# Row tiles in a pool of their own, and other banks and addresses at the start of the down stage

## The chip, the cores and the metric

The kernel runs on one core of one Trainium2 chip. The metric is device time in microseconds (us) for one execution of the whole program; less is better.

## What is computed

Two layers of a decoder trunk on an input x of 1024 rows by 1024 columns, all in float32. Each layer has a mix part (a causal convolution group and a differential attention group side by side, then one projection) and a gated feed-forward part; each adds its normalized result to x:

```python
z = jnp.einsum("bsd,dc->bsc", rms_norm(x, pre_mix_norm[l]), w_in[l])
u, o = conv_group(z), diff_attention_group(z)
m = jnp.einsum("bsc,cd->bsd", jnp.concatenate([u, o], axis=-1), w_out[l])
x = x + rms_norm(m, post_mix_norm[l])
up = jnp.einsum("bsd,df->bsf", rms_norm(x, pre_ffn_norm[l]), w_up[l])
g, val = jnp.split(causal_dwconv(up, ffn_conv_w[l], ffn_conv_b[l]), 2, axis=-1)
f = jnp.einsum("bsf,fd->bsd", jax.nn.gelu(g, approximate=True) * val, w_down[l])
x = x + rms_norm(f, post_ffn_norm[l])
```

The feed-forward width is 2816: w_up has 2 x 2816 columns, w_down 2816 rows.

## The kernel before, in words

Per layer there are three stages on TensorE: **mix**, **up** (w_up with the convolution of width 3 and the gate) and **down** (w_down). A float32 product is made of three float32r products: each operand is split in a high part (a rounded copy by ScalarE, line 1278) and a low part (the operand less the high part, by VectorE or GpSimd, line 1279), and high x high, low x high and high x low are summed in one PSUM bank. Up and down are done by a seven-product scheme (Strassen-like) on halves of the operands, which is why seven pieces f_l_j_k of the gated result are written to DRAM by up (lines 1482, 1484 and 1498, from the tiles gg and fs) and read back by down.

**Mix.** The last thing that it does on each 128-row tile is the post-norm: it fetches the row (xe), adds the normalized projection to it (lines 1165, 1166), stores it (1168), squares it (1171), scales it by the next norm's gain into xn (1178) and transposes it. Row tiles of 1024 columns have the tag e and five slots in the pool mx; the same tag serves the attention's exponentials. bst (statistics) and the query tiles ql1 and ql2 lie in the same pool.

**Up.** It begins with the loads of its convolution weights fw and fb (1269, 1271) and of the first raw weight blocks (1382), which lie where the tiles of the mix stage have been. The parts of a block are the tiles wo (seven slots). The products px, py and pz (line 1582) go to the PSUM pools pO, pS and pmm; VectorE adds them into cg and cv (1450); taps of the convolution are summed in acc (PSUM pools pmm for the gate half, ptr for the value half, 1456 and 1468); line 1478 multiplies acc and vv into gg.

**Down.** `run(j, ps, ...)` (line 1612) does product j of the seven: 11 chunks of 256 KB, each with 12 matmuls (line 1633): four row tiles tt = 0 to 3, each with its own bank ps[tt], by three part products. The operands of a chunk are the parts of a piece of f (fa, loaded by `fetch_f`, line 1550) and of a weight block (wbA, wbB or wb, loaded by `fetch`, line 1545). The parts of the first three chunks' weights are in wo slots, those of all later ones in wp slots (five, pool dn of the down stage). `prepare` (1552) makes the parts three chunks ahead. The banks come from `banks` (1687): product 1 begins in

```python
return ([pmm.tile([P, HB], F32, tag="mm", name="pd") for _ in range(2)]
        + [pS.tile([P, HB], F32, tag="S", name="pd") for _ in range(2)])
```

and four partial sums of 512 columns each, s1, u2 and vv, are kept in SBUF in the pool dn (line 1699), allocated before the wp slots. dn's tiles lie on addresses that tiles of the up stage have had, so the first instruction that writes one waits for the last reader of whatever lay there. The next layer's mix stage lies over dn's tiles in the same way: its first raw blocks (line 454) lie where s1 was; their high parts are whw (458, ScalarE), their low parts wlw (464, GpSimd), and the first products are pg (494).

The order of the instructions on TensorE, VectorE, ScalarE and GpSimd is the order in which the code issues them or, in the mix stage, a planner written out in the kernel. Nearly all DMAs go through one queue, SP, in order: one that waits holds all that stand behind it. A scheduler chooses the place of a DMA in SP's order when the program is built. A row in this text is named by the line numbers of the kernel before.

Of the kernel before, what the change touches and what calls it, by code (L numbers as in the profile page):

```python
# [9 lines left out]
F32 = mybir.dt.float32  # L10
F32R = mybir.dt.float32r
# [6 lines left out]
P = 128  # L18
D = 1024
T = 1024  # L20
DEPTH = 2
HB = 512
# [33 lines left out]
E_BUFS = 5  # L56
# [157 lines left out]
def build(tc, ap, out):  # L214
# [4 lines left out]
    def mv(dst, src):  # L219
        sy.dma_start(f32(dst), f32(src))  # L220

    with ExitStack() as top:
        def pool(st, name, **kw):
            return st.enter_context(tc.tile_pool(name=name, **kw))
# [5 lines left out]
        pmm = pool(top, "pmm", bufs=2, space=PSUM)  # L230
        pS = pool(top, "pS", bufs=3, space=PSUM)
        ptr = pool(top, "ptr", bufs=2, space=PSUM)
        pO = pool(top, "pO", bufs=1, space=PSUM)
# [182 lines left out]
        for l in range(DEPTH):  # L416
            xres = xin if l == 0 else x2[l - 1]
            with ExitStack() as st:
                mx = pool(st, f"mx{l}", bufs=1, reuse_waits="tile")
                mw = pool(st, f"mw{l}", bufs=1, reuse_waits="tile")  # L420
                hh = (hA, hB)
                if l == 0:
                    for t in range(8):
                        late[t] = prenorm(ptr, x0[t] if t < 3 else first_x(t), g_pre, hh[t // 4], t % 4)
                p = params(l)
                wm = ap["wmix"][l]

                bst = mx.tile([P, 8, 4, 6], F32, tag="bst", name="bst")
                qlow = [mx.tile([P, HB], F32R, tag=tag, name=tag) for tag in ("ql1", "ql2")]
                po.memset(f32(qlow[0][64:128]), 0.0)  # L430
                po.memset(f32(qlow[1][0:64]), 0.0)
# [2 lines left out]
                                                     e=E_BUFS, aT=AT_BUFS, osb=1, qs=1, kA=1, kB=1, v0=2, v1=2,  # L434
# [92 lines left out]
                def conv_gate(ct, b, ps, im):  # L527
                    tag = "e" if ct == 0 else "m0"
                    it = yield from R[tag].get()
                    if ct == 0:  # L530
                        tg = mx.tile([P, T], F32, tag="e", name="tg", bufs=E_BUFS)[:, 0:HB]
                    else:
                        tg = xs.tile([P, HB], F32, tag="m0", name="tg", bufs=4)
                    se.activation(tg, ps, AF.Tanh, scale=0.5)
                    t = fl.op("act", ac(HB))
                    R["mm"].free(im, t)
                    tgs[ct, b] = tg, tag, it
                    fl.set("tg", ct, b)
# [256 lines left out]
                def attn(h, b):  # L795

                    n = SEQ.index((h, b))
                    if n > 0:
                        yield ("S", SEQ[n - 1][0], 4 * SEQ[n - 1][1] + 3)
                    if b == 1:  # L800
                        yield ("kA", h)
                    yield ("qk", h, b)
                    q1, q2 = kq[h, b]
                    grp = {}
                    for qb in range(4 * b, 4 * b + 4):
                        nk = (qb + 1) * P
                        qsl = slice(qb % 4 * P, (qb % 4 + 1) * P)
                        both = []
                        for qs, ql, ki in ((q1, qlow[0], 0), (q2, qlow[1], 1)):
                            ie = yield from R["e"].get()  # L810
                            e = mx.tile([P, T], F32, tag="e", name="e", bufs=E_BUFS)
                            pcs = []
                            for c0 in range(0, nk, HB):
                                w = min(HB, nk - c0)
                                iS = yield from R["S"].get()
                                S = pS.tile([P, HB], F32, tag="S", name="S")[:, 0:w]
                                diag = c0 + w == nk
                                kt = kk[h, c0 // HB]
                                pe.matmul(S, qs[:, qsl], kt[ki][:, 0:w], start=True, stop=False)
                                pe.matmul(S, ql[:, qsl], kt[ki][:, 0:w], start=False, stop=not diag)  # L820
                                if diag:
                                    pe.matmul(S[:, w - P:w], identr, nmaskr, start=False, stop=True)  # L822
                                t = fl.op("pe", 2 * max(0.107, w / 2400) + (0.06 if diag else 0))
                                pcs.append((S, c0, w, iS))
                            fl.spawn(soft(h, qb, pcs, e, ie, both, grp), t)
                        if qb % 4 == 3:
                            R["qs"].free(ikq[h, b, "qs"], t)
                            if b == 1:
                                R["kA"].free(ikq[h, 0, "k"], t)
                                R["kB"].free(ikq[h, 1, "k"], t)  # L830
                            elif h in SPILL:
                                R["kA"].free(ikq[h, 0, "k"], t)
                        fl.set("S", h, qb)
# [121 lines left out]
                def norm(h, b, grp):  # L955
                    osb, oss, ep = grp[0]
                    po.tensor_scalar(ep, ep, EPS * P, None, op0=ALU.mult)
                    po.tensor_tensor(ep, ep, oss, op=ALU.add)
                    po.tensor_tensor(ep, ep, negh[:, 0:G], op=ALU.pow)
                    yield fl.op("pool", 1.6)  # L960
                    for qi in range(G):
                        se.activation(osb[:, qi], osb[:, qi], AF.Copy, scale=ep[:, qi:qi + 1])
                        t = fl.op("act", 0.29)
                    yield t
                    io = yield from R["e"].get()
                    onT = mx.tile([P, 2, HB], F32R, tag="e", name="onT", bufs=E_BUFS)
                    ip = yield from R["tr"].get()
                    pt = ptr.tile([P, G, P], F32, tag="tr", name="pto")
                    for qi in range(G):
                        pe.transpose(pt[:, qi], osb[:, qi], ident)  # L970
                    t = fl.op("pe", 0.48)
                    R["osb"].free(grp[1], t)
                    yield t
                    ptf = pt.rearrange("p a b -> p (a b)")
                    se.activation(onT[:, 0], ptf, AF.Copy, scale=p["sg"])
                    t = fl.op("act", ac(HB) + 0.1)
                    yield t
                    ve.scalar_tensor_tensor(onT[:, 1], ptf, p["sg"], f32(onT[:, 0]), op0=ALU.mult, op1=ALU.subtract)
                    t = fl.op("dve", dv(HB), t)
                    R["tr"].free(ip, t)  # L980
                    mv(osp[l][h][b], onT)
                    R["e"].free(io, t + MV_LAT)
                    yield t
                    fl.set("norm", h, b)
# [70 lines left out]
                m0s, xe = {}, {}  # L1055
# [55 lines left out]
                def wout_half(dh, b, tt, ps, tag, im):  # L1111
# [21 lines left out]
                    yield t  # L1133
                    if b == 1:
                        i = yield from R["e"].get()
                        x = mx.tile([P, D], F32, tag="e", name="xe", bufs=E_BUFS)
                        sy.dma_start(x, xres[4 + tt])
                        xe[tt] = x, i, fl.now + MV_LAT
                        fl.set("xe", tt)

                def wout_post(dh, b, tt, ps, tag, im):
# [4 lines left out]
                    if b == 1:  # L1146
                        if ("xe", tt) not in fl.seen:
                            yield ("xe", tt)
                        x, ie, tx = xe[tt]
                        yield from R["xr" if tt < 2 else "y"].get()  # L1150
                        xn = xs.tile([P, D if tt < 2 else YW], F32, tag="xr" if tt < 2 else "y", name="xn", bufs=2)[:, 0:D]
# [56 lines left out]
                        R["y"].free(i, t)  # L1208
                    yield ("hA2",)
                    i = yield from R["e"].get()  # L1210
                    xn = mx.tile([P, D], F32, tag="e", name="xn", bufs=E_BUFS)
                    ss = xs.tile([P, 1], F32, tag="ss", name="ss", bufs=3)
                    se.activation(xn, y, AF.Square, accum_out=ss)
                    t = fl.op("act", ac(D) + 0.1)
# [50 lines left out]
            with ExitStack() as st:  # L1265
# [36 lines left out]
                with ExitStack() as su:  # L1302
# [197 lines left out]
                    for n in range(NFT):  # L1500
                        e, f4 = slot[3, n] + 1, slot[4, n] + 1
# [107 lines left out]
                with ExitStack() as sd:  # L1609
                    dn = pool(sd, f"dn{l}", bufs=1, reuse_waits="tile")  # L1610
# [73 lines left out]
                    def keep(name):  # L1684
                        return [dn.tile([P, HB], F32, tag=name, name=name, bufs=4) for _ in range(4)]

                    def banks(which):
                        if which == 0:
                            return ([pmm.tile([P, HB], F32, tag="mm", name="pd") for _ in range(2)]
                                    + [pS.tile([P, HB], F32, tag="S", name="pd") for _ in range(2)])  # L1690
                        return ([pS.tile([P, HB], F32, tag="S", name="pd"), pO.tile([P, HB], F32, tag="o", name="pd")]
                                + [ptr.tile([P, HB], F32, tag="tr", name="pd") for _ in range(2)])

                    inB = [hpool.tile([P, 8, HB], F32, tag="hB", name="wbB") for _ in range(2)]
# [1 line left out]
                    spB = [t[:, j] for t in inB for j in range(8)]  # L1696
                    B.update({"dn": dn, "12": spB[0:K2], "22": own[1:12], "21": B["A"][K2:16] + spB[K2:16] + own[0:1]})
                    pa = banks(0)
                    s1, u2, vv = keep("s1"), keep("u2"), keep("vv")
                    m0s = {}  # L1700

                    def end1(tt):
# [126 lines left out]
```

## Time and profile before

| | us |
|---|---|
| median of 3 runs | 2388.04 (2386.19 to 2391.40) |
| the profiled execution | 2385.93 |
| its span | 2384.1 |
| TensorE busy | 2214.6 |
| TensorE's mean granted clock | 0.965 of full speed |

A busy line gives the time that an engine worked. A wait is idle time of an engine right before an instruction, with the instruction that ended it. A timeline gives the instructions of an engine in order of time, with consecutive like ones merged. Times in views are us from the start of the span.

### The profile page before, as it was taken

The numbers are of one execution on the slowest core, as the hardware profiler recorded it, in microseconds if no ns is written. First come the engines' busy times: TensorE is split into PE (matmuls) and PEld (weight loads), VectorE is DVE, ScalarE is ACT, GpSimd is POOL, SyncE is SP. The second block draws the span as 40 slices with busy tenths as digits, with TensorE's granted clock in tenths as the row PEclk, the third lists the DMA queues.
The fourth block names the chain that finished last, engine by engine and source line by source line (L and its number), as shares of the span: only waits on it lengthen the run. The fifth ranks groups of instructions, "written<-read, shape, count | busy, mean of one in ns | idle before, by whom it ended". The sixth has DMA issues, their size and how long they took to land. (4 is left out here: it accounts for less than half of the span.)

```text
span 2384.1 us, 31534 instructions
## 1 busy us (share of the span) xinstructions
PE 2214.6 (93%) x10568; PEld 1845.5 (77%) x10568; DVE 1857.6 (78%) x3285; ACT 1132.9 (48%) x2458; POOL 826.0 (35%) x896
## 2 busy tenths in 40 slices
PE   6999998959999999899869999989699999998997
PEld 4998886748877878788658988867588778787886
DVE  6889989537888888677668899885478888886777
ACT  4445556535444444444434455565354544444443
POOL 3223312234544544202432233122354555442024
PEclk9999998979999999999979999989899999999999
DMA  4313323644334334833333123236433334348343
GB/s 144 78 53 89 90 74 114 200 137 143 111 124 132 111 125 152 286 98 102 110 113 80 53 87 93 71 112 202 143 133 124 120 121 135 103 168 273 98 150 106
DMA packets 140129, 295.39 MB, mean 124 GB/s; under 512 B 16832, under 2 KB 33984, under 8 KB 139456
## 3 DMA queue, kind: packets, MB, share of 16 engines
q1 hardware_dynamic: 139968, 293.39, 38.7%
q8 instruction: 83, 1.36, 0.2%
q14 instruction: 78, 0.64, 0.1%
HBM read 198.44 MB, written 78.12 MB: 116 GB/s over the span
## 5 line engine op out<-in xcount | busy, mean ns | idle before, releaser
L1633 PE MATMUL pd<-wp,wo 128*128 128x512 f32 x1776 | 411.3, 393 | 5.5 <-DVE vv L1718 2.9
L1633 PEld LDWEIGHTS pd<-wp,wo 128*128 128x128 f32 x1776 | 336.0, 190 | 77.8 <-issue 3.3
L1582 PE MATMUL py<-t,wo 128*128 128x512 f32 x1584 | 377.5, 391 | 4.5 <-DVE cg L1450 4.5
L1582 PEld LDWEIGHTS py<-t,wo 128*128 128x128 f32 x1584 | 296.6, 188 | 73.4 <-ACT wo L1278 7.7
L1279 POOL TENSOR_TENSOR wo<-ws,wo 128x512 fp32r<-128x512 f32 x176 | 252.2, 1444 | 283.7 <-ACT wo L1278 246.6
L1582 PE MATMUL px<-hA,wo 128*128 128x512 f32 x1056 | 261.6, 400 | 43.4 <-ACT wo L1278 42.3
L1582 PEld LDWEIGHTS px<-hA,wo 128*128 128x128 f32 x1056 | 199.6, 190 | 93.4 <-ACT wo L1278 43.2
L1279 POOL TENSOR_TENSOR wo<-raw,wo 128x512 fp32r<-128x512 f32 x132 | 177.4, 1348 | 145.0 <-ACT wo L1278 142.6
L1279 POOL TENSOR_TENSOR wo<-fa,wo 128x512 fp32r<-128x512 f32 x66 | 101.4, 1552 | 328.2 <-ACT wo L1278 308.6
L1278 ACT ACTIVATE wo<-ws 128x512 fp32r<-128x512 f32 x176 | 108.5, 626 | 135.7 <-PE py L1582 57.4
L1468 DVE SCALAR_TENSOR_TENSOR acc<-cg,fw,acc 128x512 f32<-128x512 f32 x176 | 132.7, 754 | 41.7 <-ACT acc L1456 38.0
L592 DVE SCALAR_TENSOR_TENSOR scr<-u,cw,scr 128x256 f32<-128x256 f32 (+2 forms) x288 | 158.9, 572 | 0.4
L494 PE MATMUL pq<-whq,hA 128*128 128x384 f32 x512 | 138.2, 352 | 5.8 <-ACT whq L458 5.8
L1456 ACT ACTIVATE acc<-cg,fb,fw 128x512 f32<-128x512 f32 x88 | 68.2, 775 | 148.0 <-DVE cg L1450 148.0
L494 PE MATMUL pq<-whq,hB 128*128 128x384 f32 x512 | 135.6, 346 | 0.0
L1582 PE MATMUL pz<-b,wo 128*128 128x512 f32 x528 | 131.1, 397 | 2.0 <-DVE cv L1450 2.0
L1582 PE MATMUL pz<-t,wo 128*128 128x512 f32 x528 | 130.5, 396 | 0.0
L847 ACT ACTIVATE e<-S,mxv 128x512 f32<-128x512 f32 (+2 forms) x192 | 110.0, 581 | 42.9 <-DVE mxv L842 31.7
L838 DVE TENSOR_REDUCE mxv<-S 128x1 f32<-128x512 f32 (+2 forms) x192 | 100.7, 549 | 29.1 <-PE S L822 27.1
L852 POOL TENSOR_TENSOR sm<-sm 128x1 f32<-128x1 f32 x64 | 27.2, 425 | 274.7 <-ACT e L847 274.7
L1582 PEld LDWEIGHTS pz<-b,wo 128*128 128x128 f32 x528 | 98.3, 188 | 28.4 <-issue 5.4
L1582 PEld LDWEIGHTS pz<-t,wo 128*128 128x128 f32 x528 | 99.0, 188 | 23.6
(279 smaller groups left out, 5003.7 us busy)
## 6 DMA issues: line engine op xcount, KB each, us to landing
raw<-in_wupd SPq DMA_DIRECT2D x104, 512.0 KB, 3.7
fa<-f SPq DMA_DIRECT2D x154, 256.0 KB, 2.7
f<-fs SPq DMA_DIRECT2D x88, 256.0 KB, 3.4
raw<-in_wmix SPq DMA_DIRECT2D x80, 256.0 KB, 2.9
f<-gg SPq DMA_DIRECT2D x66, 256.0 KB, 2.0
raw<-in_wmix SPq DMA_DIRECT2D x64, 192.0 KB, 2.5
qs<-sth SPq DMA_DIRECT2D x64, 128.0 KB, 2.8
os<-onT SPq DMA_DIRECT2D x16, 512.0 KB, 2.9
```

Source lines behind the costliest of these rows:

```text
L494: mm = pe.matmul(dst, a, b, start=first and k + j == 0, stop=final and k == n - 1 and j == 2)
L592: ve.scalar_tensor_tensor(dst, src, wk, dst, op0=ALU.mult, op1=ALU.add)
L838: ve.tensor_reduce(mv_[:, j:j + 1], S, axis=AX.X, op=ALU.max, negate=True)
L847: se.activation(e[:, c0:c0 + w], S, AF.Exp, bias=mv_[:, 0:1], accum_out=sm[:, j:j + 1])
L852: po.tensor_tensor(sm[:, 0:1], sm[:, 0:1], sm[:, 1:2], op=ALU.add)
L1278: se.activation(w[:, 0], raw, AF.Copy)
L1279: eng.tensor_tensor(w[:, 1], raw, f32(w[:, 0]), op=ALU.subtract)
L1456: se.activation(acc[n, v, hf], C[n][v][:, 2 + hf * HB:2 + hf * HB + HB], AF.Identity, bias=fb[:, mt:mt + 1], scale=fw[:, mt, 2:3])
L1468: ve.scalar_tensor_tensor(dst, c[:, j + hf * HB:j + hf * HB + HB], fw[:, mt, j:j + 1], a, op0=ALU.mult, op1=ALU.add)
L1582: pe.matmul(ps, x, y, start=first and k + j == 0, stop=k == 3 and j == 2, skip_group_check=not first)
L1633: pe.matmul(ps[tt], x, y, start=first and k + n == 0, stop=k == K2 - 1 and n == 2, skip_group_check=not first)
```

## The change

Three edits. (1) The row tiles (tag e) move out of the pool mx into a pool of their own, me, allocated behind it, and bst is given 480 columns a partition where it uses 192. (2) `banks(0)` returns one bank of pO and three of pS in place of two of pmm and two of pS; `banks(1)` two of pmm and two of ptr in place of one of pS, one of pO and two of ptr. (3) In the pool dn, u2 and vv come first, then the five wp slots (five tiles that nothing uses fix their place), then s1.

```diff
@@ mix stage
                 mx = pool(st, f"mx{l}", bufs=1, reuse_waits="tile")
+                me = pool(st, f"me{l}", bufs=1, reuse_waits="tile")
                 mw = pool(st, f"mw{l}", bufs=1, reuse_waits="tile")
...
-                bst = mx.tile([P, 8, 4, 6], F32, tag="bst", name="bst")
+                bst = mx.tile([P, 480], F32, tag="bst", name="bst")[:, 0:192].rearrange("p (a b c) -> p a b c", a=8, b=4)
...
-                            e = mx.tile([P, T], F32, tag="e", name="e", bufs=E_BUFS)
+                            e = me.tile([P, T], F32, tag="e", name="e", bufs=E_BUFS)
...
-                        x = mx.tile([P, D], F32, tag="e", name="xe", bufs=E_BUFS)
+                        x = me.tile([P, D], F32, tag="e", name="xe", bufs=E_BUFS)
...
-                    xn = mx.tile([P, D], F32, tag="e", name="xn", bufs=E_BUFS)
+                    xn = me.tile([P, D], F32, tag="e", name="xn", bufs=E_BUFS)
@@ down stage
                         if which == 0:
-                            return ([pmm.tile([P, HB], F32, tag="mm", name="pd") for _ in range(2)]
-                                    + [pS.tile([P, HB], F32, tag="S", name="pd") for _ in range(2)])
-                        return ([pS.tile([P, HB], F32, tag="S", name="pd"), pO.tile([P, HB], F32, tag="o", name="pd")]
+                            return ([pO.tile([P, HB], F32, tag="o", name="pd")]
+                                    + [pS.tile([P, HB], F32, tag="S", name="pd") for _ in range(3)])
+                        return ([pmm.tile([P, HB], F32, tag="mm", name="pd") for _ in range(2)]
                                 + [ptr.tile([P, HB], F32, tag="tr", name="pd") for _ in range(2)])
...
-                    s1, u2, vv = keep("s1"), keep("u2"), keep("vv")
+                    u2, vv = keep("u2"), keep("vv")
+                    for _ in range(5):
+                        dn.tile([P, 2, HB], F32R, tag="wp", name="wp", bufs=5)
+                    s1 = keep("s1")
```

The other two tiles of tag e (tg and onT) change pool in the same way. No instruction is added or removed, and TensorE, VectorE and ScalarE keep their order. Two queues change theirs. The first is SP at the beginning of each layer's down stage, here layer 0 (names end in a buffer number; f_1_10 is the last piece of product 1, the pieces f_2_k are those of product 2; lines of the changed kernel are one higher). Before:

```order
320 L1550 DMA fa<-f_1_9_180 128x512
321 L1545 DMA wbB<-in_wupd 128x512
322 L1550 DMA fa<-f_1_10_181 128x512
323 L1545 DMA wbB<-in_wupd 128x512
324 L1550 DMA fa<-f_2_0_182 128x512
325 L1545 DMA wbB<-in_wupd 128x512
326 L1550 DMA fa<-f_2_1_183 128x512
327 L1545 DMA wbB<-in_wupd 128x512
328 L1545 DMA wb<-in_wupd 128x512
329 L1545 DMA wbB<-in_wupd 128x512
330 L1550 DMA fa<-f_2_2_184 128x512
331 L1545 DMA wbB<-in_wupd 128x512
```

And in the changed kernel:

```order
320 L1551 DMA fa<-f_1_9_180 128x512
321 L1551 DMA fa<-f_1_10_181 128x512
322 L1546 DMA wbB<-in_wupd 128x512
323 L1551 DMA fa<-f_2_0_182 128x512
324 L1551 DMA fa<-f_2_1_183 128x512
325 L1551 DMA fa<-f_2_2_184 128x512
326 L1546 DMA wbB<-in_wupd 128x512
327 L1551 DMA fa<-f_2_3_185 128x512
328 L1546 DMA wbB<-in_wupd 128x512 x2
329 L1546 DMA wb<-in_wupd 128x512
330 L1551 DMA fa<-f_2_4_186 128x512
331 L1546 DMA wbB<-in_wupd 128x512 x2
```

The loads of pieces f_1_10 to f_2_6 have moved ahead of weight blocks wbB 11 to 16 and wb 1 to 12; everything on SP ahead of these rows stands as before.

The second queue is GpSimd at the start of layer 1's mix stage. Before:

```order
293 L1279 TENSOR_TENSOR wo<-fa,wo 128x512 x8
294 L351 TENSOR_TENSOR rs<-ss,negh 128x1 x5
295 L430 MEMSET ql_11441 64x512
296 L431 MEMSET ql_11442 64x512
297 L464 TENSOR_TENSOR wlw<-raw,whw 128x512 x4
```

And in the changed kernel:

```order
293 L1280 TENSOR_TENSOR wo<-fa,wo 128x512 x8
294 L351 TENSOR_TENSOR rs<-ss,negh 128x1 x2
295 L431 MEMSET ql_11453 64x512
296 L432 MEMSET ql_11454 64x512
297 L351 TENSOR_TENSOR rs<-ss,negh 128x1 x3
298 L465 TENSOR_TENSOR wlw<-raw,whw 128x512 x4
```

The two memsets of ql1 and ql2 have moved ahead of three of the small operations that make the norm's factors.

## Rows read from the trace of the kernel before

**Rows 1.** Waits of TensorE: waiting line, releaser, total us, times, longest.
```profile
PE px L1582 <- ACT wo L1278: 42.3, 2, 23.3
...
PE pd L1633 <- DVE gg L1478: 13.9, 2, 6.9
PE pg L494 <- ACT whw L458: 12.4, 1, 12.4
```

**Rows 2.** Timeline of SP, end of layer 0's mix stage: start, us, instruction, [idle before].
```profile
515.42 0.33 SPq L246 DMA_DIRECT2D gb<-in_norms  x1
...
516.96 2.78 SPq L1382 DMA_DIRECT2D raw<-in_wupd  x4
```

**Rows 3.** Timeline of TensorE, start of layer 0's up stage.
```profile
522.47 0.79 PE L1582 MATMUL px<-hA,wo 128*128 128x512 f32 x1 [23.30 <-ACT wo L1278]
```

**Rows 4.** Timeline of SP, start of layer 1's up stage.
```profile
1705.29 3.08 SPq L1382 DMA_DIRECT2D raw<-in_wupd  x4
```

**Rows 5.** Timeline of TensorE, from up to down in layer 0.
```profile
958.48 2.92 PE L1582 MATMUL py<-t,wo 128*128 128x512 f32 x12
968.33 10.98 PE L1633 MATMUL pd<-wo 128*128 128x512 f32 x36 [6.93 <-DVE gg L1478]
979.15 6.06 PE L1633 MATMUL pd<-wp,wo 128*128 128x512 f32 x26
```

**Rows 6.** Timeline of VectorE, from up to down in layer 0.
```profile
954.79 1.36 DVE L1279 TENSOR_TENSOR wo<-wbA,wo 128x512 fp32r<-128x512 f32 x1 [3.00 <-ACT wo L1278]
...
958.12 0.68 DVE L1279 TENSOR_TENSOR wo<-wbA,wo 128x512 fp32r<-128x512 f32 x1
958.72 0.68 DVE L1450 TENSOR_TENSOR cg<-pz,cg 128x512 f32<-128x512 f32 x1
...
961.81 1.34 DVE L1279 TENSOR_TENSOR wo<-wbA,wo 128x512 fp32r<-128x512 f32 x1
963.07 0.68 DVE L1450 TENSOR_TENSOR cv<-py,cv 128x512 f32<-128x512 f32 x1
...
967.50 1.28 DVE L1478 TENSOR_TENSOR gg<-acc,vv 128x512 f32<-128x512 f32 x2
...
971.36 0.68 DVE L1279 TENSOR_TENSOR wp<-wbA,wp 128x512 fp32r<-128x512 f32 x1
```

**Rows 7.** Timeline of GpSimd, the same stretch.
```profile
954.32 1.29 POOL L1279 TENSOR_TENSOR wo<-fa,wo 128x512 fp32r<-128x512 f32 x1 [7.86 <-DMA f<-gg]
...
966.38 1.27 POOL L1279 TENSOR_TENSOR wo<-fa,wo 128x512 fp32r<-128x512 f32 x1 [3.78 <-ACT wo L1278]
```

**Rows 8.** Stretches: us, busy time (and instructions) per engine, PEclk, DMA share, GB/s.
```profile
968.33:974.00 5.67, 5.67 (x14) 4.47 (x15) 3.64 (x6) 0.12 (x1) 0.00 (x0) 0.51 0.96 351
```

**Rows 9.** The same view, behind a pause of 2.06 us in layer 1's down stage.
```profile
2331.15:2335.76 4.61, 4.61 (x13) 3.70 (x14) 4.61 (x3) 2.35 (x5) 4.11 (x3) 0.63 0.81 249
```

**Rows 10.** Line 1484 from 968.5 to 969.5: its two stores, issue to landing.
```profile
DMA to landing us min/median/max: 5.4/5.5/5.6
```

**Rows 11.** Timeline of SP, layer 0's down stage: the last wb loads.
```profile
995.31 0.90 SPq L1545 DMA_DIRECT2D wb<-in_wupd  x2
```

**Rows 12.** Timeline of TensorE, from up to down in layer 1.
```profile
2156.09 11.05 PE L1633 MATMUL pd<-wo 128*128 128x512 f32 x36 [6.93 <-DVE gg L1478]
```

**Rows 13.** Timeline of SP, start of layer 1's mix stage.
```profile
1202.42 0.32 SPq L405 DMA_DIRECT2D x<-y  x1
1206.93 5.21 SPq L454 DMA_DIRECT2D raw<-in_wmix  x4
```

**Rows 14.** Timeline of ScalarE, start of layer 1's mix stage.
```profile
1206.18 0.63 ACT L391 ACTIVATE y<-s 128x512 f32<-128x512 f32 x1 [1.04 <-DVE nl L298]
...
1209.75 0.63 ACT L458 ACTIVATE whw<-raw 128x512 fp32r<-128x512 f32 x1 [2.85 <-DMA raw<-in_wmix]
```

**Rows 15.** Timeline of GpSimd, the same stretch.
```profile
1200.03 0.92 POOL L351 TENSOR_TENSOR rs<-ss,negh 128x1 f32<-128x1 f32 x1 [2.13 <-DVE ss L349]
...
1205.07 0.52 POOL L430 MEMSET ql<- 64x512 f32 x1
```

More of the change, by code (lines that the diff above doesn't have):

```diff
@@ L530, in conv_gate @@
                     if ct == 0:
-                        tg = mx.tile([P, T], F32, tag="e", name="tg", bufs=E_BUFS)[:, 0:HB]
+                        tg = me.tile([P, T], F32, tag="e", name="tg", bufs=E_BUFS)[:, 0:HB]
                     else:
@@ L965, in norm @@
                     io = yield from R["e"].get()
-                    onT = mx.tile([P, 2, HB], F32R, tag="e", name="onT", bufs=E_BUFS)
+                    onT = me.tile([P, 2, HB], F32R, tag="e", name="onT", bufs=E_BUFS)
                     ip = yield from R["tr"].get()
```

## The prediction

> **What bounds the kernel.** I read the waits of TensorE first, since it is the busy engine and only its idle time can come back. Three of its waits stand where the change touches addresses or banks [rows 1]: the first up products wait for the parts of raw weights (42.3 us in two layers), the first down products for VectorE's gg (13.9, 6.9 each), the first products of layer 1's mix for whw (12.4). Then, at each of the three places, I read the timelines of the engine that released it and of its queue, to see what would be late next if the wait were gone. Last, the granted clock: after a pause TensorE works at half speed, 1.2 instead of 2.4 GHz (14 matmuls in 5.67 us at 0.51 of full speed behind the 6.93 us pause [rows 8]; at full speed 26 take 6.06 [rows 5], 0.23 each, so 14 would take 3.2).
>
> **Mix to up: nothing.** The row tiles lay where the raw weights of up go, and in a pool of their own they no longer hold those loads. But the loads stand in SP's order behind a load of gb that leaves at 515.42, and they leave at 516.96, right after it and the two convolution loads [rows 2]; the first product comes 5.5 later, at 522.47 [rows 3]. The gb load keeps its place in the order and its buffer (the pool of norm gains is not touched). In layer 1 the first raw load leaves at 1705.29 [rows 4] as the last of the same row of loads, with no row tile's wait of its own ahead of the product that ends the 19.0 us pause (42.3 less 23.3); the second load might leave about 1.3 us sooner, but is needed some 5 us after the first. From both sides: 0 at least, and 42.3 at most if my reading of the queue is wrong. I take 0, the value of the two SP rows.
>
> **Up to down: about 5.35 us a layer.** The last up product ends at 961.4 (958.48 + 2.92) and the first pd at 968.33 [rows 5]. It waits for the pmm banks of tt 0 and 1, in which acc lies until gg has read it (967.50 to 968.78 [rows 6]). Its operands had long been there: the low parts of the first three chunks' weights end at 956.15, 958.80 and 963.15 [rows 6]. With the new banks, tt 0 and 1 find theirs free, the bank of tt 2 is free after cg<-pz (959.40), that of tt 3 after cv<-py (963.75) [rows 6]. Step by step:
> - chunk 0: nine matmuls (tt 0 to 2) by 961.4 + 9 x 0.23 = 963.5; a short wait for tt 3 to about 963.9;
> - the other 27 of chunks 0 to 2: 27 x 0.23 = 6.2, to 970.1;
> - chunk 3 needs the first wp, whose low part is VectorE's row at 971.36, done 972.04 [rows 6]. VectorE's work ahead of it (taps, gg, fs) doesn't wait for TensorE's down products, so it stays. That is **what is late next**: chunk 3 starts about 972.2 in place of 979.15 [rows 5], 6.95 sooner.
>
> Against that goes the clock. A pause of 2.1 us (970.1 to 972.2) is left. Behind a pause of 2.06 us elsewhere, 13 matmuls took 4.61 us at 0.63 [rows 9] where 13 x 0.23 = 3.0 would do: 1.6 lost. Bounds: 0, or the 2.5 (5.67 - 3.2) that the long pause costs [rows 8]. I take 1.6, since the pause is of the same length; 6.95 - 1.6 = 5.35, between 4.45 and 6.95. Layer 1 has the same rows 1187.8 us later (a pause of 6.93, then 36 matmuls in 11.05 [rows 12]), so twice: 10.7.
>
> GpSimd splits chunk 3's f at 966.38 [rows 7]; its split of chunk 4 waited for TensorE to let go of a wo slot and now comes at once behind it, to about 968.9, beside gg and fs on VectorE. One row shows what such company does: the low part at 954.79 took 1.36 us beside a GpSimd split (954.32 to 955.61 [rows 7]), that at 958.12 took 0.68 alone [rows 6]. I count up to 0.7 a layer as a bound and 0 in the sum, as only the fs right behind gg, from 968.8 on, would meet it, for its first tenth of a microsecond. The Trainium skill (SBUF — State Buffer, Who interferes with whom) has a rule for this, that a VectorE instruction with two SBUF inputs contends with a GpSimd instruction that reads SBUF. The trace agrees (1.36 beside, 0.68 alone); with a full block at that point the sum would be 1.4 us smaller, which changes no case.
>
> **The later supply: nothing.** The wp slots move: the second and third now lie where gg lay, so their parts wait for fs (done by 971.4, when the first wp starts) and for two stores of gg, issued from about 968.5 and landed 5.4 to 5.6 us later [rows 10], 974.7. ScalarE is held there, with the f parts of chunks 5 to 7 queued behind it. Chunk 5 is ready about 2.1 us behind the landing (a copy of 0.6, a low part of 0.7 to 1.4), at 976.8. TensorE takes 12 x 0.23 = 2.76 a chunk, so it asks for chunk 5 at 972.2 + 2 x 2.76 = 977.7, or at 979.3 if slow: 0.9 to 2.5 to spare. What SP moves back, blocks wbB 11 to 16 and wb 1 to 12, is wanted from chunk 16 on, prepared three chunks ahead, at 972.2 + 10 x 2.76 = 999.8 at the earliest; the last of all 12 wb left at 995.31 to 996.2 before [rows 11], wanted only from chunk 21 on. The f loads now ahead of them come early too, since their slots are let go sooner. Cost 0; a bound of 2 a layer.
>
> **Down to mix of layer 1: 2.8 us.** The first raw loads of the mix lay on s1. They leave at 1206.93, 4.2 us after the store ahead of them (1202.42 + 0.32) [rows 13], when ScalarE (1206.18 + 0.63 [rows 14]) and VectorE have read the last s1. Over u2 and vv, done with much earlier, they leave at 1202.75 and are there for ScalarE by 1205.6 (1209.75 - 1206.93 = 2.82 later). ScalarE has the row at 1206.18 ahead of the copy in its order, so whw starts near 1206.95 in place of 1209.75 [rows 14]: 2.8, and everything behind shifts along. GpSimd's two memsets move into idle time of 2.13 us ahead of the row at 1200.03 and take 0.52 each [rows 15]: 0. Bounds 0 to 2.8; I take 2.8.
>
> **Sum.** 10.7 + 2.8 = 13.5. The profiled execution took 2385.93, 2.1 under the median of the runs; 2385.93 - 13.5 = 2372.4, and from the median 2388.04 - 13.5 = 2374.5. The worst of the bounds (4.45 - 0.7 - 2 a layer, mix 0) gives 3.5, the best (6.95 twice, 2.8) 16.7.
>
> **Rivals.**
> - *Part is given back* (chance 0.13): chunks 4 to 6 come late, because the DMA queues are nearly full there (351 GB/s [rows 8]) and a store that held nobody now holds ScalarE, or the low clock lasts longer. For it: only 0.9 us to spare. Against: the landings are those of before, as nothing ahead of them moves. Gain 5 to 9: 2379 to 2383.
> - *Mix to up opens too* (0.05): if the row tiles, not the gb load, held the raw loads. They could then go after about 509, 8 us sooner in layer 0, and as much in layer 1: 13.5 + 16 = 29.5, 2358.5; 2332 if all of 42.3 went. Against it: the order on SP [rows 2].
> - *The change doesn't do what it says at the border* (0.06): a first pd still waits for something as late as gg, so only the mix's 2.8 comes: 2385.2. Against it: no reader of the new banks is later than 963.75 [rows 6].
> - *Slower* (0.04): the wait for gg's stores takes the place of the wait for gg. It decides from the landing of those stores: harmless to 975.6, then each microsecond delays TensorE by one; from 975.6 + 6.75 = 982.4 it has eaten 13.5 / 2 a layer. With a landing at 986 the loss is 2 x 10.4 - 13.5 = 7.3: 2395.3. That takes 17 us in flight where the rows show 5.4 to 5.6 [rows 10].
>
> **How the numbers follow.** The forecast (gain 10 to 17) has 0.72. The range reaches from the best of the bounds, less 3 for the spread of runs (2386.19 to 2391.40), 2368, to the middle of the first rival and a little beyond, 2382; outside lie the second to fourth rivals and the tail of the first, 2 in 10 at most. A measurement of this kernel tells some 0.2%, 4.8 us, from no change: faster takes the forecast, the first rival and the second, 0.72 + 0.13 + 0.05 = 0.90; same 0.06; slower 0.04.
>
> **What would show it.** Right: TensorE's wait for gg is gone from the waits; the pause between py and pd is under 0.5 us, a second one of about 2 us stands ahead of the first pd<-wp with VectorE's wp as releaser, and the first pd<-wp starts about 3.4 us behind the end of gg (968.78), in place of 10.4; pg starts 2.8 sooner after the last pd; the 42.3 us stays. Wrong: that wait falls, a wait of pd on ScalarE's or VectorE's wp beyond 3 us a layer, or new waits on wb in the later chunks.

## The result, and the profile after

The changed kernel takes 2363.65 us (median of 4 runs, 2362.74 to 2370.43) against 2387.93 for the kernel before in the same runs; the ratio is 0.9903, with a 95% interval of 0.9881 to 0.9924. That is 24 us faster, 18 to 28 by the interval; forecast were 13.5, with a range that ended at 2368. The direction was right, the size was not. The profiled execution took 2363.12 us with a span of 2361.0, 23.1 under the span before.

TensorE issues the same products in the same order in both kernels, so the two traces can be laid side by side product by product. Stretches run from the start of the first product named to the start of the next stretch:

| stretch | before | after | difference |
|---|---|---|---|
| start of the span to the first transpose | 14.0 | 13.1 | -0.9 |
| mix of layer 0, with the pause behind it | 508.4 | 508.6 | +0.1 |
| up of layer 0, to the first pd | 445.9 | 439.4 | -6.5 |
| the first 36 pd | 10.8 | 8.9 | -2.0 |
| the rest of down, with the pause ahead of layer 1's mix | 231.3 | 229.3 | -2.0 |
| mix of layer 1, with the pause behind it | 499.4 | 496.4 | -3.0 |
| up of layer 1, to the first pd | 446.2 | 439.5 | -6.8 |
| the first 36 pd | 10.9 | 8.9 | -2.0 |
| the rest of down, to its last product | 206.0 | 206.1 | 0.0 |

The waits of TensorE in the changed kernel (lines are one or a few higher than before):

```profile
PE px L1583 <- ACT wo L1279: 42.1, 2, 23.1
...
PE pg L495 <- ACT whw L459: 9.3, 1, 9.3
...
PE pd L1634 <- DVE wp L1280: 4.9, 3, 2.1
...
PE pd L1634 <- DVE cv L1451: 0.8, 2, 0.4
```

Against [rows 1], the wait for gg is gone, the wait for whw is 3.0 shorter (12.37 and 9.34), and that of px is what it was. The wait for wp, which before came once with 2.1, now comes three times; a small one for cv is new. **From up to down**, TensorE's timeline in layer 0, beside [rows 5]:

```profile
958.27 2.92 PE L1583 MATMUL py<-t,wo 128*128 128x512 f32 x12
961.03 2.20 PE L1634 MATMUL pd<-wo 128*128 128x512 f32 x9
963.62 6.42 PE L1634 MATMUL pd<-wo 128*128 128x512 f32 x27 [0.39 <-DVE cv L1451]
969.87 0.61 PE L1634 MATMUL pd<-wp,wo 128*128 128x512 f32 x2
971.91 18.47 PE L1634 MATMUL pd<-wp,wo 128*128 128x512 f32 x80 [1.42 <-DVE wp L1280]
```

Nine products, a short wait for the bank of tt 3, 27 more, and then a pause for the first wp: the steps of the prediction, to within 0.3 us. But two products of chunk 3 come ahead of the pause, which is 1.42 us and not 2.1. The granted clock (the third figure from the end of a row, behind POOL) stays full across it, in layer 1 as well, where the prediction had it fall:

```profile
969.87:971.91 2.04, 0.62 (x3) 0.19 (x1) 2.04 (x5) 1.15 (x2) 0.00 (x0) 1.00 1.00 361
971.91:976.00 4.09, 4.09 (x18) 3.36 (x19) 1.41 (x3) 1.88 (x4) 2.35 (x2) 1.00 1.04 356
```

The pause of 2.06 us from which the prediction took the price of the clock [rows 9] is still there, ahead of the same product of layer 1's down stage. It is as long as before, but now the clock stays full behind it: 20 matmuls in 4.61 us, where 13 had taken as long.

```profile
2309.54 10.76 PE L1634 MATMUL pd<-wp,wo 128*128 128x512 f32 x46 [2.05 <-DVE wp L1280]
```

```profile
2309.54:2314.15 4.61, 4.61 (x20) 3.79 (x21) 4.61 (x3) 2.47 (x5) 4.26 (x4) 1.00 0.80 238
```

VectorE, ScalarE and GpSimd at the border of layer 0, one fence each:

```profile
968.63 0.69 DVE L1498 TENSOR_TENSOR fs<-gg 128x512 f32<-128x512 f32 x1
969.36 0.69 DVE L1498 TENSOR_TENSOR fs<-fs,gg 128x512 f32<-128x512 f32 x1
...
971.17 1.28 DVE L1280 TENSOR_TENSOR wp<-wbA,wp 128x512 fp32r<-128x512 f32 x2
```

```profile
970.69 0.63 ACT L1279 ACTIVATE wp<-wbA 128x512 fp32r<-128x512 f32 x1 [3.53 <-DVE fs L1498]
971.23 0.61 ACT L1279 ACTIVATE wo<-fa 128x512 fp32r<-128x512 f32 x1
974.12 0.63 ACT L1279 ACTIVATE wp<-wbA 128x512 fp32r<-128x512 f32 x1 [2.28 <-DMA f<-gg]
```

```profile
966.20 2.55 POOL L1280 TENSOR_TENSOR wo<-fa,wo 128x512 fp32r<-128x512 f32 x2 [3.79 <-ACT wo L1279]
971.92 1.70 POOL L1280 TENSOR_TENSOR wo<-fa,wo 128x512 fp32r<-128x512 f32 x1 [3.16 <-DMA f<-gg]
```

ScalarE stands 3.53 us at the second wp, until the third of the four fs is done, and 2.28 at the third wp, until the stores of gg have landed. Both waits stand in the prediction's part on the later supply; the slower rival rested on the second. TensorE doesn't feel them, and meanwhile GpSimd, which needs ScalarE's copies, stands too: its split at 971.92 follows the copy of 971.23, though its row names a DMA as the releaser. What that is worth, the experiments show.

**From down to mix**, ScalarE and then TensorE, beside [rows 13, 14] and the 12.4 of [rows 1]:

```profile
1197.85 0.63 ACT L391 ACTIVATE y<-s 128x512 f32<-128x512 f32 x1 [0.97 <-DVE nl L298]
...
1198.48 1.91 ACT L459 ACTIVATE whw<-raw 128x512 fp32r<-128x512 f32 x3
```

```profile
1199.15 0.80 PE L495 MATMUL pg<-hA,whw 128*128 128x512 f32 x1 [9.34 <-ACT whw L459]
```

The copy into whw follows ScalarE's work on s directly, as forecast. **In the mix stage** a product has become shorter, which nothing in the prediction provides for. One group of its products, from 440 to 499 us (minimum, median and longest duration in ns), before and after:

```profile
L494 PE MATMUL pw<-whq,cat x80: 390/393/477, 441.1 to 498.5; 128*128 128x512 f32 x80
```

```profile
L495 PE MATMUL pw<-whq,cat x80: 389/389/477, 441.7 to 497.9; 128*128 128x512 f32 x80
```

Products overlap, so what counts is from start to start: a median of 232 ns before and 227 after at full clock, over the 254 of this group in both layers, and likewise for the other products with cat and hB (pq, with 384 columns, 175 and 174).

### The profile page after: what moved, and what is told of

The parts are those of the page before. It is cut to its first block, busy times and chain, and to the rows that moved or that the text cites. A ratio compares the mean times of both kernels' runs of the same rounds, so it can differ in the third digit from the quotient of the medians.

```text
span 2361.0 us, 31535 instructions
## 1 busy us (share of the span) xinstructions
PE 2203.4 (93%) x10568; PEld 1837.9 (78%) x10568; DVE 1857.8 (79%) x3285; ACT 1131.9 (48%) x2458; POOL 827.4 (35%) x896
## 5 line engine op out<-in xcount | busy, mean ns | idle before, releaser
L1583 PE MATMUL px<-hA,wo 128*128 128x512 f32 x1056 | 262.6, 401 | 43.3 <-ACT wo L1279 42.1
```

What stands on the lines that cost most here:

```text
L1583: pe.matmul(ps, x, y, start=first and k + j == 0, stop=k == 3 and j == 2, skip_group_check=not first)
```

## The experiments

Thirteen kernels ran; each ratio is to the kernel before in the same set of runs, with its 95% interval.

**1. The banks alone** (edit 2 of the change, word for word as in its diff).

> Only the banks of down's products are changed (edit 2). Theory A (the banks are worth 7.3 us a layer, because the pause that is left ahead of chunk 3 leaves the clock at full speed): 14 to 15 us faster than the kernel before, 2373 to 2374; the 36 products of chunks 0 to 2 take some 8.9 us where they took 10.8, and the wait for gg is gone. Rival B (the clock falls behind the short pause as the prediction had it, and the rest of the measured gain comes from the moved wp slots): about 10.7 us faster, 2377, with a stretch at half clock behind the first down products.

2381.16 us against 2388.05, ratio 0.9972 (0.9962 to 0.9981): 6.9 faster, less than either theory. VectorE, then GpSimd, then TensorE of this kernel:

```profile
973.48 0.69 DVE L1497 TENSOR_TENSOR fs<-gg 128x512 f32<-128x512 f32 x1
974.21 1.66 DVE L1497 TENSOR_TENSOR fs<-fs,gg 128x512 f32<-128x512 f32 x1
975.79 1.75 DVE L1497 TENSOR_TENSOR fs<-gg 128x512 f32<-128x512 f32 x1
977.46 0.68 DVE L1497 TENSOR_TENSOR fs<-gg,fs 128x512 f32<-128x512 f32 x1
```

```profile
971.04 5.95 POOL L1279 TENSOR_TENSOR wo<-fa,wo 128x512 fp32r<-128x512 f32 x4 [3.78 <-ACT wo L1278]
```

```profile
974.72 0.61 PE L1633 MATMUL pd<-wp,wo 128*128 128x512 f32 x2
978.80 11.44 PE L1633 MATMUL pd<-wp,wo 128*128 128x512 f32 x42 [3.47 <-DVE wp L1279]
```

Here the second and third wp don't lie over gg, ScalarE isn't held at them, and GpSimd makes four splits in a row from 971.04 to 976.99. Two of the four fs take 1.66 and 1.75 beside them in place of 0.69, 2.0 us together (the first, which starts as a split ends, still takes 0.69), and the pause ahead of the first wp is 3.47 in place of 1.42. Behind this longer pause the clock does fall: 13 matmuls in 4.60 us at 0.63 of full speed.

```profile
978.80:983.40 4.60, 4.60 (x13) 3.63 (x14) 3.45 (x4) 0.63 (x1) 1.69 (x1) 0.63 0.93 302
```

Layer 1 shows the same (a pause of 3.47, fs of 1.66 and 1.75). The pause is 2.05 longer, and with 13 x 0.23 = 3.0 for the same work the clock costs 1.6: 3.65 a layer. The whole change brings 14.5 at the two borders (worked out below); less 7.3 that leaves 7.2, about the 6.9 measured.

**2. The place of s1 alone** (edit 3).

> Only the place of s1 in the down stage's pool is changed (edit 3). Theory A: 3.1 us faster, 2385, all of it at the start of layer 1's mix stage, where the wait of pg for whw falls from 12.4 to 9.3; the 6.9 us waits for gg stay. Rival B (the moved wp slots also bring the later chunks sooner, or hold ScalarE for the stores of gg): the down stage's own time changes by over 1 us a layer.

2386.00 against 2388.05, ratio 0.9989 (0.9980 to 0.9998): 2.0 faster, 0.5 to 4.8 by the interval. The wait for whw is 9.4; the waits for gg stay at 13.9.

**3. The row tiles' pool alone**, with bst at 192 columns (the `me` lines of edit 1 without the line on bst).

> Only the row tiles' own pool (edit 1), with bst at its old 192 columns, so that the weight parts of the mix stage keep their old addresses. Theory A (the pool itself is worth nothing, since the raw loads stand behind the gb load on SP): within 1 us of the kernel before, 2387 to 2389; the 42.3 us of waits stay, and a pw product at full clock still takes 232 ns from start to start. Rival B (the row tiles' new place is what makes the mix stage's products faster): 2.5 us faster and 228 ns.

2387.43 against 2388.05, ratio 1.0000 (0.9990 to 1.0009): nothing, as theory A has it. The products with cat have a median of 393 ns, as before.

**4. The wider bst alone.**

```diff
-                bst = mx.tile([P, 8, 4, 6], F32, tag="bst", name="bst")
+                bst = mx.tile([P, 480], F32, tag="bst", name="bst")[:, 0:192].rearrange("p (a b c) -> p a b c", a=8, b=4)
```

> Only bst is widened from 192 to 480 columns, which moves every tile behind it in the mix stage by 1152 bytes, the weight parts among them. Theory A (the products of the mix stage take 232 or 228 ns from start to start by the address of the weight parts): 228 ns for pw and 173 for pq where they took 232 and 176, and 2 to 3 us faster, 2385 to 2386. Rival B (the faster products come with the row tiles' pool, or are a spread between runs): 232 and 176 ns, no change of the time.

2381.42 against 2388.05, ratio 0.9973 (0.9963 to 0.9983): 6.6 faster, more than twice what was expected, by two effects. The products are faster:

```profile
L494 PE MATMUL pw<-whq,cat x82: 387/389/477, 440.0 to 498.8; 128*128 128x512 f32 x82
```

And the 1152 bytes also move layer 1's first raw block off the s1 tile that is read last, so the wait for whw falls to 9.4 here as well. SP's raw loads leave right behind the store (1203.85 + 0.32):

```profile
1203.85 0.32 SPq L405 DMA_DIRECT2D x<-y  x1
1204.26 8.82 SPq L454 DMA_DIRECT2D raw<-in_wmix  x6
```

So edits 1 and 3 each bring these 3 us, and together bring them once. By subtraction, about 3.6 is left to the faster products.

**5. Banks and place of s1 together.**

> The banks and the place of s1 (edits 2 and 3), without the row tiles' pool and the wider bst. Theory A (the two edits need each other: the wp slots over gg hold ScalarE at the second wp until fs is done, so that GpSimd has no split to run beside fs and the first wp is ready 2 us sooner than with the banks alone): 17 to 18 us faster than the kernel before, about 2370; an fs takes 0.69 us, the pause ahead of chunk 3's low part is about 1.4 us. Rival B (the effects only add up, 6.9 and 2.0): 9 us faster, 2379, with fs of 1.7 us as with the banks alone.

2371.64 against 2388.11, ratio 0.9927 (0.9913 to 0.9942): 16.5 faster, where the two alone add up to 8.9. All four fs take 0.68 to 0.69 us, and the pause is 1.42 again. Theory A holds.

**6. Banks alone, without GpSimd beside fs.** To tell GpSimd's company from the wp slots' addresses, which both differ between the first and the fifth run:

```diff
-                        x = parts(fa.pop(c), po if j in (1, 7, 4) else ve)
+                        x = parts(fa.pop(c), po if j in (1, 7, 4) and c not in (4, 5, 6) else ve)
```

> The banks alone, as in the first run, with the low parts of the f pieces of chunks 4 to 6 made by VectorE (in its order behind the first wp) and not by GpSimd, so that GpSimd has nothing to do beside fs; the wp slots keep their old places. Theory A (GpSimd's splits beside fs made the first wp 2 us late): an fs takes 0.69 us, the pause ahead of chunk 3's low part is 1.4 us and not 3.5, the clock stays at 2.4 GHz, and the time is 12 to 15 us under the kernel before, 2373 to 2376, less what VectorE's three added operations cost. Rival B (the old places of the wp slots themselves make the first wp late): fs of 1.7 us and 2381 as before.

2375.09 against 2386.99, ratio 0.9947 (0.9931 to 0.9964): 11.9 faster, with the wp slots where they were. VectorE, and TensorE behind it:

```profile
973.51 0.69 DVE L1497 TENSOR_TENSOR fs<-fs,gg 128x512 f32<-128x512 f32 x1
974.12 0.69 DVE L1497 TENSOR_TENSOR fs<-gg 128x512 f32<-128x512 f32 x1
974.72 0.69 DVE L1497 TENSOR_TENSOR fs<-gg,fs 128x512 f32<-128x512 f32 x1
975.32 0.69 DVE L1279 TENSOR_TENSOR wp<-wbA,wp 128x512 fp32r<-128x512 f32 x1
```

```profile
976.06 14.14 PE L1633 MATMUL pd<-wp,wo 128*128 128x512 f32 x61 [1.41 <-DVE wp L1279]
```

It is GpSimd's company that makes fs slow, not the addresses. The Trainium skill (SBUF — State Buffer, Who interferes with whom) says that a VectorE instruction with two SBUF inputs contends with a GpSimd instruction that reads SBUF; the trace agrees, at 0.69 us alone and 1.66 to 1.75 beside four splits in a row.

**7. The whole change without the wider bst.**

> The whole change but for the wider bst, which stays at 192 columns. Theory A (the width moves the weight parts of the mix stage by 1152 bytes, and the products take 228 in place of 232 ns from start to start): 2 to 4 us slower than the whole change, 2366 to 2368, pw at 232 ns, while the wait of pg for whw stays at 9.3. Rival B (the faster products belong to the row tiles' pool or the other edits): the time of the whole change, 2363.7, and 228 ns.

2369.82 against 2388.11, ratio 0.9922 (0.9907 to 0.9936), 6.2 slower than the whole change by the medians (its ratio, 0.9903, was taken in other runs). The products are back at 393 ns, and the wait for whw stays short, as theory A has it:

```profile
L495 PE MATMUL pw<-whq,cat x79: 390/393/477, 439.8 to 498.8; 128*128 128x512 f32 x79
```

In this profile a further 2.9 us were lost late in layer 1's down stage, in waits for wp and a stretch at half clock; they are in no other run with edits 2 and 3, so part of the 6.2 may be theirs.

**8 to 10. What holds the raw loads of up.** The prediction read from [rows 2] that the gain load on SP holds them. Eight: the loads of g_pf and of the next layer's g_pre go through ScalarE's queue.

```diff
-                    g_pf = gvec(l, 3)
+                    g_pf = gvec(l, 3, se)
+                    g_next = None if last else gvec(l + 1, 0, se)
```

> The whole change, and the two loads of norm gains that stand ahead of up's raw loads on SP go through ScalarE's queue, late in the up stage. If these loads hold the raw loads, as the prediction's rows say: in layer 0 the raw loads leave right behind the store of the last row tile, 3.5 us sooner, and in layer 1, where the store and not the gain load is last, no sooner: 3.5 us faster than the whole change, 2360. If the row tiles' addresses or something else holds them: the wait of 42.1 us stays and the time too.

2363.20 against 2388.11, ratio 0.9891 (0.9876 to 0.9906). The raw loads leave at 513.26 (516.34 with the whole change), and the pause is 3.3 shorter; the time hardly falls:

```profile
PE px L1583 <- ACT wo L1279: 38.8, 2, 19.8
```

What is won there is lost again at the border to down. The second gain load now stands in ScalarE's order ahead of a tap of the convolution, and ScalarE stands 3.34 us until that load can go, at 960.51; ahead of the same tap it stood 2.03 in the changed kernel. So the taps, gg, fs and the first wp come 1.3 us later, and the pause ahead of that wp is 2.73 us in place of 1.42:

```profile
960.51 0.33 ACTq L246 DMA_DIRECT2D gb<-in_norms  x1
960.89 1.49 ACT L1457 ACTIVATE acc<-cv,fb,fw 128x512 f32<-128x512 f32 x2 [3.34 <-DMA wbA<-in_wupd]
```

```profile
969.21 15.96 PE L1635 MATMUL pd<-wp,wo 128*128 128x512 f32 x62 [2.73 <-DVE wp L1280]
```

Behind it the clock falls (14 matmuls in 4.79 us at 0.64).

Nine: the store of the late row tiles, too.

```diff
-                        sy.dma_start(x1[l][4 + tt], x)
...
                         se.activation(xn, x, AF.Square, accum_out=ss)
+                        se.dma_start(x1[l][4 + tt], x)
```

> As the run before, and the stores of the four late row tiles go through ScalarE's queue too, so that nothing late is ahead of up's raw loads on SP. If SP's order alone held them: the raw loads leave some 10 us sooner, the first product then waits for ScalarE's copy, which stands behind its last square of a row tile: about 8.5 us sooner in layer 0 and 4 in layer 1, 12 in sum, 2351, the wait of px at about 30. If the loads of up now disturb the end of the mix stage (its row tiles come through the same transfers): less than 6 us.

2357.71, ratio 0.9873 (0.9856 to 0.9889). SP, ScalarE and the wait:

```profile
501.90 22.47 SPq L1383 DMA_DIRECT2D raw<-in_wupd  x6
```

```profile
511.07 1.06 ACT L1171 ACTIVATE xn<-xe 128x1024 f32<-128x1024 f32 x1 [2.60 <-DVE xe L1167]
...
512.13 3.73 ACT L1279 ACTIVATE wo<-raw 128x512 fp32r<-128x512 f32 x7
```

```profile
PE px L1583 <- ACT wo L1279: 29.5, 2, 14.9
```

The raw loads leave 14.4 us sooner and the first wo now waits for ScalarE alone: 12.6 us of waits are gone. That the row tiles' own pool is needed for this isn't shown, since no run moved the loads without it. Still, in both runs the rest of layer 0's down stage is 3 to 4 us longer (232.2 and 233.2 against 229.3). Ten: as nine, with the gain loads in the middle of the up stage.

> As the run with gain loads and row stores on ScalarE's queue, but the gain loads are issued in the middle of the up stage and not at its end, where the transfers are full. Theory (the 2 to 4 us that layer 0's down stage grew by in that run came from these loads beside the weight and f loads): the rest of layer 0's down stage is back to about 229.3 us from 233.2, and the time falls by 2 to 4 us, to about 2355. Rival (the down stage of that run was longer by chance, or by the earlier start): no change, 2357 to 2358.

2352.32 against 2387.47, ratio 0.9850 (0.9835 to 0.9865), 5.4 under run nine; the rest of layer 0's down stage is 229.2 again. In run eight the whole loss lay at the border, where ScalarE stood at its own gain load; with the loads moved it stands 2.03 us ahead of that tap again. Of run nine's 3.9 only 1.2 lies at the border; ScalarE's load doesn't hold it there, but its third wp waits 5.36 us for a store (1.81 in run ten), and TensorE 0.69 for that. The other 2.7 come late in the stage, from 1108 us on, at a mean clock of 0.88 (0.93 with the whole change, 0.97 in run ten). Run eleven, which moves no load, has a like stretch of 0.88 there and loses 2.4, so these 2.7 can't be put down to the gain loads. That the loads stood beside other transfers isn't shown.

**11 and 12. Where an operand lies.** The built program puts cat, hA, t1 and b22 at addresses that are 96 above a multiple of 256 bytes in a partition; the mix stage's weight parts lay at 224 above one before, and at 96 with the wider bst. In up, wo lies at 64 above a multiple: against t2 to t4 the distance is a multiple of 256, against hA, t1 and b22 it is not. The profile of the changed kernel from 600 to 800 us has just that difference:

```profile
L1583 PE MATMUL py<-t,wo x401: 387/389/467, 599.6 to 794.5; 128*128 128x512 f32 x134
...
L1583 PE MATMUL px<-hA,wo x179: 393/394/397, 603.6 to 799.9; 128*128 128x512 f32 x179
...
L1583 PE MATMUL pz<-b,wo x144: 392/396/470, 600.8 to 797.3; 128*128 128x512 f32 x144
```

The edit moves all tiles behind fb (8 columns are 32 bytes; 24 in run 12):

```diff
-                fb = fw_.tile([P, 2 * NFT], F32, tag="fb", name="fb")
+                fb = fw_.tile([P, 2 * NFT + 8], F32, tag="fb", name="fb")[:, 0:2 * NFT]
```

> The whole change, and every tile of the up and down stages 32 bytes further (fb is 8 columns wider). Theory (a matmul takes 227 ns from start to start when the addresses of its two operands in a partition differ by a multiple of 256 bytes, and 232 to 234 otherwise; wo now lies 224 above such a multiple against hA, t1 and b22): px and pz fall from 234 to 227 ns, and py, whose operands move together, is to rise in no product (its operands keep their distance, 227): 2112 products by 7 ns, some 14 us faster than the whole change, 2349. Rival (the absolute address of the weights counts): px and pz stay at 234.

2355.39, ratio 0.9870 (0.9854 to 0.9887), 8.3 under the whole change by the medians. From start to start px and pz fall from 234 to 227 ns, and their durations in the same stretch are those of py:

```profile
L1583 PE MATMUL px<-hA,wo x180: 389/389/389, 602.3 to 796.2; 128*128 128x512 f32 x180
L1583 PE MATMUL pz<-b,wo x143: 387/389/470, 599.8 to 793.5; 128*128 128x512 f32 x143
```

The up stages are 6.5 and 6.0 us shorter, not 14 in sum: the waits of py for VectorE's cg grew from 4.5 to 7.9. Of these 12.5 us, 2.4 go again in layer 0's down stage, in the late stretch at a lower clock named above.

> As the run before with 96 bytes in place of 32, so that wo lies 64 above a multiple of 256 against hA, t1 and b22. Theory (distance a multiple of 256): px and pz at 232 to 234 ns, the time of the whole change, 2363 to 2364. Rival (a multiple of 64 is enough): 227 ns and 14 us faster.

2364.18, ratio 0.9903 (0.9888 to 0.9918): the time of the whole change. With a distance of 64 above a multiple of 256 the products stay slow:

```profile
L1583 PE MATMUL px<-hA,wo x174: 393/394/398, 604.9 to 799.8; 128*128 128x512 f32 x174
```

**13. All together**: runs ten and eleven in one kernel.

> The whole change with the gain loads in the middle of up, the row stores on ScalarE's queue and the 32 bytes. If the gains add up: 8 to 9 us from the queues and 14 from the addresses, 2340 to 2342. If the faster products only uncover the splits of the up stage's weights (ScalarE and GpSimd): 2345 to 2352, with waits of px and pz on wo that were not there.

2339.38 against 2387.47, ratio 0.9803 (0.9788 to 0.9817): 48 us under the kernel before and 24 under the changed one, the fastest of the study. Two of its waits, against 42.1 and 4.5 with the whole change:

```profile
PE px L1591 <- ACT wo L1279: 29.2, 2, 14.6
...
PE py L1591 <- DVE cg L1451: 7.9, 8, 1.0
```

## Why the prediction was wrong in size

- **What bounds the kernel, and that nothing comes from mix to up**: right. The wait of px is 42.1, and the pool alone is worth nothing. Runs eight to ten show the reason that the rows gave: the order on SP.
- **Up to down, the steps to chunk 3**: right. The first wp is done at about 971.9 (forecast 972.04), and what is late next is VectorE's low part of it.
- **The clock term, -1.6 a layer**: this step failed. I counted a pause of 2.1 us and took the price of one of 2.06 elsewhere. The pause is 1.42, since the first two products of chunk 3 need only the high part of the weights, and the granted clock stayed at 1.00 behind it in both layers. So the term of 5.35 a layer, 10.7 in sum, was mis-sized: by the table it measured 6.5 + 2.0 - 1.4 = 7.1 and 6.8 + 2.0 - 1.4 = 7.4, 14.5 in sum. Nor was the length of a pause enough to tell its price. That other pause, 2.01 to 2.06 us in every profile, has 0.63 to 0.64 behind it in the four kernels with the old banks (before and runs 2 to 4) and 1.00 in all with the new banks but run 7, which has another pause of 2.0 just ahead. Behind the longer ones, 2.73 (run 8) and 3.47 (run 1), it was 0.64 and 0.63. What decides between the levels at about 2 us stays open.
- **The later supply, nothing**: right in its sum, but for a reason that the working missed. I saw that ScalarE would be held for fs and for the stores and looked only for harm. Holding ScalarE until fs is nearly done also stops GpSimd, and that keeps VectorE's fs at 0.69 us. Without it (run 1) the banks lose half of their worth; with GpSimd's work taken away by other means (run 6) they keep most of it. The company term, 0 to 0.7 a layer beside the first fs, was right for this kernel and shows what it can grow to: 2.0.
- **Down to mix, 2.8**: right, 3.0 measured. That bst's width alone would do it too, I did not see.
- **A term that is missing**: this step failed as well. The prediction doesn't name bst's width and so puts it at nothing without a reason. The mix stage's products went from 232 to 227 ns, some 3.6 us by run 4 with the border's 3 taken off, and up to 6 by run 7. In the two profiles shown, layer 1's mix is 3.0 shorter and layer 0's isn't shorter at all, since its waits grew by 3.4 us in this pair. It decides the range: the change without the width (run 7) measured 2369.82, inside it, and with the clock term at its bound of 0 the sum would have been 16.7, some 2369 to 2371, inside it too.
- The rest, 1.6, is the stretch at half clock of [rows 9], which the profile after doesn't have. It goes with the banks, as said above; by what way isn't shown.

So 14.5 + 3.0 + 3.0 + 1.6 = 22.1 of the 23.1 by which the spans differ; 0.9 lies ahead of the first product.

## What to carry to other kernels

An engine that waits may be keeping out of another's way: before counting a hold as harm or as nothing, ask what the held engine would run beside, and try edits alone and together, since two that bring 6.9 and 2.0 alone brought 16.5. Freeing an address frees a load only if nothing ahead of it in its queue is late; look up the queue's order at once. A load that is moved to a computing engine's queue can hold that engine, as in run 8, so choose its place there too. A price read behind one pause need not hold behind the next of the same length. And compare the median duration of like products between two kernels before explaining a difference by waits: a tile's width can be a change of rate.

## What was not expected of the hardware

A float32r matmul of 128x512 takes 227 ns from start to start where the addresses of its two operands in a partition differ by a multiple of 256 bytes, and 232 to 234 at distances of 64, 128 and 224 above such a multiple; those are the distances that were tried. In some of the products early in the mix stage (pg and pa) the changed kernel has the right distance and still 228 to 231; why is open. The effect is worth 3.6 to 6 us in the mix stages and 8 to 13 in the up stages of this kernel.
